# Output weights and results loaded a unit or more ahead of their split, keys stored regrouped, one bias sum for two column tiles

## The chip, the cores and the metric

The kernel runs on one core of one Trainium2 chip. The core has a TensorE (PE, with its weight loads shown apart as PEld), a VectorE (DVE), a ScalarE (ACT), a GpSimd (POOL) and a SyncE (SP) whose queue starts most transfers. Each engine executes its own instructions strictly in the order in which they stand in the program; between engines, semaphores make one wait for another. The metric is the device time in microseconds (us); lower is better.

## What is computed

One layer of an image backbone, on 1024 latent tokens (16 rows of 64 columns), 256 context tokens and 1024 features. A projection of the modulated input gives two parallel mixers; the output projection joins them.

```python
# 1. neighbourhood attention: 8 heads of 64, window of 8 rows x 16 columns, learned bias, plus all context keys
s_loc = jnp.einsum('bchd,bicjhd->bhcij', q_r, k_win).astype(jnp.float32) + bias
s_ctx = jnp.einsum('bchd,bnhd->bhcn', q_r, k_ctx).astype(jnp.float32)
s = jnp.concatenate([s_loc.reshape(B, H, GRID_W, kh * NA_KW), s_ctx], axis=-1)
p = jax.nn.softmax(s, axis=-1).astype(v.dtype)
...
# 2. gated DeltaNet: 4 heads of 128, chunked scan, forward and backward in time
v_new = u_n - jnp.einsum('bhcd,bhde->bhce', w_n, state)
o_n = (jnp.einsum('bhcd,bhde->bhce', q_n, state)
       + jnp.einsum('bhij,bhje->bhie', qk_n, v_new))
state = state * gl_n[..., None, None] + jnp.einsum('bhcd,bhce->bhde', k_n, v_new)
...
# 3. both gated, joined, projected; normalised residual
y = jnp.concatenate([o_na * jax.nn.silu(na_z), o_g * jax.nn.silu(g_z)], axis=-1) @ w_out
x = x + gate[:, None] * rmsnorm(y, g_post)
```

All arithmetic has the precision of fp32. Matrix products run as two or three products of operands that are split in a high and a low part, so each weight and each result is "split": ACT copies the rounded high part, another engine subtracts it from the original to get the low one.

## The kernel before

The program has two parts. Up to about 554 us come the projections, the convolution, the scan's triangular inverses and all that feeds the mixers; the change touches there only `qk_out`, which splits queries and keys of attention and stores them in `qk_dram`. The rest is `phase_b`, and it is the part of interest.

**Attention** (`na_attn`, `na_unit`) runs over 4 pairs of heads (p), 2 row tiles (rt) and 4 column tiles (ct): 32 units of 128 queries, two heads each. Per head of a unit: POOL adds relative bias and mask into `gm` (L676; 288 columns for ct 0 and 3, 384 for 1 and 2); TensorE makes scores with the context keys, `pc` (L684), and with the window's keys, `pl` (L688); DVE takes a maximum `mi` (L692) and adds the bias (L693, giving `pt` and `nm`); ACT takes the exponentials (L694, L695); TensorE transposes them (L697, L702), DVE and ACT copy them out (`tl` L699, `tcx` L704); TensorE makes the output `po` (L710, L715). `pc` and `pl` have two buffers each. After four units `po` is scaled by the gate in `zs` and the sums' reciprocal `rb`, which TensorE transposes as `prt` (L621). The keys lie row by row in `kk`, so the window of a unit is read as columns 64 elements apart.

**The scan** (`delta_scan`) runs over 4 heads (h), 10 chunks, both directions d together. A step is a chain: TensorE `pa` with the state (L1133), DVE `y` (L1134), TensorE with the inverse `tm` (L1138), ACT `vn` (L1140, L1142), TensorE with the decayed keys `kd` (L1144), DVE the new state `s` (L1147), and beside it two matmuls for the output, `pos` (L1152, L1153). POOL makes `kd` and `vb` (L1125, L1128). After the last step of a head its result `o` is squared (L1170), normalised, transposed as `ot` (L1182) and gated in `zg`.

**The output projection** (`phase4`) multiplies eight tiles of results m by eight tiles of output weights: 384 matmuls `py` of 512 columns (L1218 to L1220). The order of the tiles k is `W_ORDER = [3, 0, 1, 2, 4, 5, 6, 7]`; tile 3 is the last pair of attention, tile 7 the last head of the scan. Results of earlier pairs and heads come back from `m_dram` into `mr` and are split (ACT L1205); the last pair's is split from `zs` by `split_m` (L659, L660). The weights are split in pieces of 128x512 by `split_w`: a load into a raw buffer `wor`, of which there are two, an ACT copy (L647) and a POOL subtract (L648). Five tiles are split inside attention and the scan (`w_out_early`, into buffers `qh`, `ql`, `kk`, `o`, `tm` that are free by then), three in `phase4` (`fintm`, `finkq`, `wh`).

`phase_b` writes attention and scan interleaved: after unit u it has written min(43, 1.40 u) scan steps (a head is ten steps and a beginning and an end). That is only the order of writing. The program is then scheduled: a list scheduler with its own model of durations takes, for each engine, what it believes to be ready, and this fixes the order on each engine. Where buffers of two pools share addresses, the later user waits for the earlier.

Of the kernel before, what the change touches and what calls it, by code (L numbers as in the profile page):

```python
# [11 lines left out]
F32 = mybir.dt.float32  # L12
# [8 lines left out]
P = 128  # L21
# [118 lines left out]
class K:  # L140
    def __init__(self, tc, I, out, dbg=None):
        self.tc, self.nc, self.I, self.out = tc, tc.nc, I, out
        self.dbg = dbg or {}
        self.na_first = None
        self.gate = self.after = None
# [371 lines left out]
    def qk_out(self, p, i, gr, src):  # L517
        nc = self.nc
        n, scale, c0 = 512 if gr < 2 else CT, 1.0 if i else 0.125, S * i + 512 * gr
        src, rows = src[:, :n], slice(P * p, P * p + P)  # L520
        hi, lo = (self.wp.tile([P, 512], F32R, name=f"s{c}_{'qk'[i]}{p}{gr}", tag="st", bufs=4)[:, :n] for c in "hl")
        nc.scalar.activation(hi, src, AF.Copy, scale=scale)
        nc.vector.scalar_tensor_tensor(lo, src, scale, hi.bitcast(F32), ALU.mult, ALU.subtract)
        nc.sync.dma_start(self.qk_dram[0, rows, c0:c0 + n], hi.bitcast(F32))
        nc.sync.dma_start(self.qk_dram[1, rows, c0:c0 + n], lo.bitcast(F32))
# [59 lines left out]
    def na_attn(self, na, ps):  # L585
# [55 lines left out]
    def split_w(self, k, hi, lo):  # L641
        nc = self.nc
        hr, lr = hi.bitcast(F32R), lo.bitcast(F32R)
        for o in range(0, D, 512):
            raw = self.g3.tile([P, 512], F32, name=f"wor{k}_{o}", tag="wor", bufs=2)
            self.load(raw, self.I["w_out"][k * P:(k + 1) * P, o:o + 512], self.na_last)
            nc.scalar.copy(hr[:, o:o + 512], raw)  # L647
            nc.gpsimd.tensor_tensor(lr[:, o:o + 512], raw, hi[:, o:o + 512], ALU.subtract)  # L648
        self.wo[k] = (hr, lr)
# [13 lines left out]
    def na_unit(self, ps, p, rt, ct, qk, vv, gts, mk, sums, po):  # L663
# [7 lines left out]
        for hh in range(2):  # L671
# [3 lines left out]
            gm = self.nw.tile([P, 384], F32, name=f"gm{p}_{u}_{hh}", tag="gm", bufs=2)  # L675
            nc.gpsimd.tensor_tensor(gm[:, :n].rearrange("p (n c r) -> p n c r", c=nco, r=4), gv,  # L676
                                    mk[:, mo:mo + n].rearrange("p (n c r) -> p n c r", c=nco, r=4), ALU.add)
# [3 lines left out]
            pl3 = pl[:, :n].rearrange("p (n c r) -> p n c r", c=nco, r=4)  # L681
            qs, kk = qk[hh]
            for i, a in enumerate(qs):
                nc.tensor.matmul(pc, a[:, u * P:(u + 1) * P], kk[:, S:S + CT], start=(i == 0), stop=(i == 1))  # L684
            kv = kk[:, 256 * rt:256 * rt + 768].rearrange("p (n r c) -> p n c r", c=64, r=4)[
                :, :, KCOL0[ct]:KCOL0[ct] + nco, :]
# [8 lines left out]
            nc.scalar.activation(pt[:, 384:640], pc, AF.Exp, bias=nm, accum_out=sums[:, ct, hh, 1:2])  # L695
# [496 lines left out]
    def phase4(self, p4, ps, last):  # L1192
# [7 lines left out]
        for k in W_ORDER:  # L1200
            if k not in self.ms and k != 7:
                raw = raws[:, D * (k % 2):D * (k % 2) + D]
                mh, ml = (tl(c, k).bitcast(F32R) for c in ("mh", "ml"))
                nc.sync.dma_start(raw, self.m_dram[k * P:(k + 1) * P, :])
                nc.scalar.copy(mh, raw)  # L1205
                nc.vector.tensor_tensor(ml, raw, mh.bitcast(F32), ALU.subtract)
                self.ms[k] = (mh, ml)
            if k not in self.wo and k != 7:
                self.split_w(k, *late[k])
# [12 lines left out]
        for tg in range(0, 8, 4):  # L1222
# [101 lines left out]
    def phase_b(self):  # L1324
        tc = self.tc
        g3 = self.g3
        self.wos, self.wo, self.ms = [], {}, {}
# [66 lines left out]
```

## Time and profile before

| | |
|---|---|
| three runs | 906.75, 904.99, 906.35 us; median 906.35 |
| profiled execution | 904.01 us, span 902.3 us, mean granted TensorE clock 0.963 of full |
| projections and inverses | up to about 554 us |
| attention with the scan | 554 to 791.8 us |
| output projection | 791.8 to 895.3 us |
| normalisation and store of the last tile | 895.3 to 902.3 us |

The span is the time from the first to the last instruction of one profiled execution; 1.7 us lie around it. Rows of the profile name a line of the kernel, the engine, the operation, and output and input by their names in the program. In rows that group instructions, the number after x is their count, then follow the busy time in us, the mean duration in ns and, behind the second bar, the idle time of the engine just before them and who ended it. In rows of a timeline the first number is the start in us and the second the duration. Rows of windows have the busy time and count of each engine in turn, then the granted TensorE clock (PEclk), then the share of the DMA engines.

### The profile page before, as it was taken

The numbers are of one execution on the slowest core, as the hardware profiler recorded it, in microseconds if no ns is written. First come the engines' busy times: TensorE is split into PE (matmuls) and PEld (weight loads), VectorE is DVE, ScalarE is ACT, GpSimd is POOL, SyncE is SP. The second block draws the span as 40 slices with busy tenths as digits, with TensorE's granted clock in tenths as the row PEclk, the third lists the DMA queues.
The fourth block names the chain that finished last, engine by engine and source line by source line (L and its number), as shares of the span: only waits on it lengthen the run. The fifth ranks groups of instructions, "written<-read, shape, count | busy, mean of one in ns | idle before, by whom it ended". The sixth has DMA issues, their size and how long they took to land.

```text
span 902.3 us, 16602 instructions
## 1 busy us (share of the span) xinstructions
PE 848.5 (94%) x6082; PEld 708.7 (79%) x6082; DVE 537.6 (60%) x1179; ACT 416.2 (46%) x1165; POOL 369.6 (41%) x431
## 2 busy tenths in 40 slices
PE   6999999999999989998998998999999988998996
PEld 4688887887788767787887877888887876887785
DVE  3463454456545699689428634677777775662442
ACT  5262525545645445652334444555545656532310
POOL 1432322614543532455241124568557569423210
PEclk9999999999999989999998985999999998999898
DMA  9786432346355534733799699949387152132351
GB/s 343 257 290 228 150 107 74 114 157 199 89 198 185 138 122 151 216 99 112 249 265 265 219 281 413 267 117 296 141 208 272 48 183 76 47 117 94 108 183 60
DMA packets 95176, 160.98 MB, mean 178 GB/s; under 512 B 28581, under 2 KB 55542, under 8 KB 92918
## 3 DMA queue, kind: packets, MB, share of 16 engines
q1 hardware_dynamic: 87606, 146.25, 51.2%
q10 hardware_dynamic: 7488, 13.67, 4.9%
q8 instruction: 48, 0.79, 0.4%
q14 instruction: 34, 0.28, 0.1%
HBM read 110.82 MB, written 52.42 MB: 181 GB/s over the span
## 4 chain that ended last, share of the span: by engine, by line
PE 64%; DVE 13%; DMA 9%; ACT 5%; issue 4%; POOL 2%; SPq 2%; ACTq 0%; DVEq 0%; POOLq 0%
PE py L1218 3%; PE py L1219 3%; PE py L1220 3%; DVE tb L1003 3%; PE pl L688 2%; DVE vb L1006 2%; PE po L715 2%; PE pl L697 2%; PE pz L464 2%; PE pc L684 2%; PE pz L460 2%; PE pz L465 2%; PE po L710 2%; PE pa L1138 2%; PE pa L1144 2%
## 5 line engine op out<-in xcount | busy, mean ns | idle before, releaser
L676 POOL TENSOR_TENSOR gm<-gt,mk 128x288 f32<-128x288 f32 (+1 forms) x64 | 64.3, 1009 | 36.0 <-DVE nm L693 35.9
L1125 POOL TENSOR_SCALAR kd<-kt,kd 128x128 f32<-128x128 f32 x72 | 43.4, 606 | 35.3 <-PE pa L1144 33.7
L694 ACT ACTIVATE pt<-pt,nm 128x288 f32<-128x288 f32 (+1 forms) x64 | 36.7, 574 | 35.7 <-DVE nm L693 35.5
L945 ACT ACTIVATE em<-em,gc 128x128 f32<-128x128 f32 x80 | 25.5, 391 | 38.2 <-DMA em<-gc_dram 32.3
L693 DVE CUSTOM_DVE_ANT_0 pt<-pl,gm,mi 128x288 f32<-128x288 f32 (+1 forms) x64 | 36.1, 564 | 11.5 <-PE pl L688 4.9
L699 DVE COPY tl<-pl 96x384 f32<-96x384 f32 (+1 forms) x64 | 35.3, 551 | 10.2 <-PE pl L697 9.9
L692 DVE TENSOR_REDUCE mi<-pc 128x1 f32<-128x256 f32 x64 | 26.8, 420 | 22.0 <-PE pc L684 21.1
L464 PE MATMUL pz<-hl,wh_gz 128*128 128x512 f32 x96 | 38.6, 402 | 0.0
L460 PE MATMUL pz<-hh,wh_gz 128*128 128x512 f32 x96 | 38.4, 400 | 0.0
L465 PE MATMUL pz<-hh,wl_gz 128*128 128x512 f32 x96 | 38.3, 399 | 0.0
L473 PE MATMUL pv<-wh_nv,hh 128*128 128x264 f32 x128 | 35.5, 295 | 2.5 <-ACT hh L262 1.7
L964 POOL TENSOR_SCALAR_AFFINE_SELECT qe<-qe 128x256 f32<-128x256 f32 x32 | 26.9, 840 | 25.8 <-DVE qe L963 25.8
L475 PE MATMUL pv<-wl_nv,hh 128*128 128x264 f32 x128 | 35.7, 286 | 1.5 <-POOL wl_nv L446 1.5
L474 PE MATMUL pv<-wh_nv,hl 128*128 128x264 f32 x128 | 36.5, 289 | 0.0
L1003 DVE TENSOR_TENSOR tb<-ab,vb 120x31 f32<-120x31 f32 (+15 forms) x62 | 32.1, 518 | 6.8 <-DMA ab<-ab_dram 5.1
L960 DVE SCALAR_TENSOR_TENSOR pm<-pk,beta,em 128x128 f32<-128x128 f32 x80 | 23.6, 343 | 19.9 <-PE pk L953 12.3
L697 PE MATMUL pl<-c,pt 128*96 128x128 f32 (+1 forms) x192 | 33.7, 285 | 1.4 <-ACT pt L694 1.2
L812 DVE SCALAR_TENSOR_TENSOR acc_v<-xp_v,cols,acc_v 128x1282 f32<-128x1282 f32 x16 | 27.5, 1719 | 9.0 <-ACT acc_v L810 8.9
L1138 PE MATMUL pa<-y,tm 128*128 128x128 f32 x144 | 29.1, 287 | 2.8 <-DVE y L1134 2.2
L1266 ACT ACTIVATE finv<-py 128x512 f32<-128x512 f32 x16 | 9.5, 599 | 46.8 <-PE py L1220 28.3
L1128 POOL TENSOR_SCALAR vb<-v,beta 128x128 f32<-128x128 f32 x40 | 24.2, 606 | 16.7 <-DVE y L1134 10.6
L704 ACT COPY tcx<-pc 128x256 f32<-128x256 f32 x64 | 23.8, 372 | 15.3 <-PE pc L702 15.1
(438 smaller groups left out, 2928.8 us busy)
## 6 DMA issues: line engine op xcount, KB each, us to landing
wada<-in_w_ada SPq DMA_DIRECT2D x16, 512.0 KB, 9.1
em<-gc_dram SPq DMA_DIRECT2D x20, 256.0 KB, 4.6
pm_dram<-pm SPq DMA_DIRECT2D x20, 256.0 KB, 3.3
pmf<-pm_dram SPq DMA_DIRECT2D x8, 640.0 KB, 8.0
tm_dram<-tm SPq DMA_DIRECT2D x8, 640.0 KB, 7.0
kk<-qk_dram SPq DMA_DIRECT2D x16, 320.0 KB, 7.9
tm<-tm_dram SPq DMA_DIRECT2D x4, 1280.0 KB
kq_dram<-kq SPq DMA_DIRECT2D x4, 1152.0 KB
```

The source lines that it names most:

```text
L460: r = nc.tensor.matmul(ps, wh, xh, start=(k == 0), stop=False)
L464: nc.tensor.matmul(ps, wh, xl, start=False, stop=False)
L465: nc.tensor.matmul(ps, wl, xh, start=False, stop=(k == KC - 1))
L474: nc.tensor.matmul(ps, xl, wh, start=False, stop=False)
L475: nc.tensor.matmul(ps, xh, wl, start=False, stop=(k == KC - 1))
L676: nc.gpsimd.tensor_tensor(gm[:, :n].rearrange("p (n c r) -> p n c r", c=nco, r=4), gv, mk[:, mo:mo + n].rearrange("p (n c r) -> p n c r", ...
L693: nc.vector.tensor_tensor_reduce(pt[:, :n], pl[:, :n], gm[:, :n], -1.0, mi, ALU.add, ALU.min, nm)
L694: nc.scalar.activation(pt[:, :n], pt[:, :n], AF.Exp, bias=nm, scale=-1.0, accum_out=sums[:, ct, hh, 0:1])
L697: nc.tensor.transpose(pl[:m, rc * P:(rc + 1) * P], pt[:, rc * m:(rc + 1) * m], self.ident)
L1003: nc.vector.tensor_tensor(t3, bc(ab[:, 0:m, m:m + 1], [r, m, n]), bc(vb[:, m:m + 1, m:], [r, m, n]), ALU.mult)
L1125: nc.gpsimd.tensor_scalar(kd, kt_[:, t, :], self.kd[:, h, d, t:t + 1], None, ALU.mult)
L1138: nc.tensor.matmul(pa, tm[:, d, t, :], y, start=True, stop=True)
```

## The change

It does four things.

1. `qk_out` stores the latent part of the keys regrouped, so that the four rows of a column stand together, and `na_unit` reads its window as one contiguous run per group of rows. For that ACT and DVE read eight groups of 512 keys from PSUM in a strided order.
2. The bias sum `gm` is not made for ct 2; units ct 1 and ct 2 share that of ct 1. 48 sums are left of 64, and `gm` has three buffers instead of two.
3. `split_w` only lists the pieces of a weight tile. `load_pieces` keeps up to two raw pieces loaded ahead, and `split_piece` splits the oldest. It is called once after each unit, so that the pieces listed at the end of pair 2 are split one a unit in pair 3, and twice in `phase4`, with two and six pieces. Its ACT copy is ordered behind the last exponential written.
4. `phase4` loads four results ahead, into four buffers, and splits them by a generator that is advanced once a tile; the rest of the scan (`last`) is written ahead of the fifth tile instead of the sixth.

```diff
+        kv = lambda v, o: v.rearrange(f"p (n {o}) -> p n c r", r=4, c=64) if i and gr < 2 else v
+        nc.scalar.activation(kv(hi, "c r"), kv(src, "r c"), AF.Copy, scale=scale)
...
@@ na_attn: after each unit
+                    self.split_piece()
                     yield
...
     def split_w(self, k, hi, lo):
-        for o in range(0, D, 512):
+        self.wo[k] = (hi.bitcast(F32R), lo.bitcast(F32R))
+        self.pieces.extend((k, o, hi[:, o:o + 512], lo[:, o:o + 512]) for o in (0, 512))
+        self.load_pieces()
+
+    def load_pieces(self):
+        while self.pieces and len(self.staged) < 2:
+            k, o, hi, lo = self.pieces.pop(0)
             raw = self.g3.tile([P, 512], F32, name=f"wor{k}_{o}", tag="wor", bufs=2)
             self.load(raw, self.I["w_out"][k * P:(k + 1) * P, o:o + 512], self.na_last)
-            nc.scalar.copy(hr[:, o:o + 512], raw)
-            nc.gpsimd.tensor_tensor(lr[:, o:o + 512], raw, hi[:, o:o + 512], ALU.subtract)
+            self.staged.append((raw, hi, lo))
+
+    def split_piece(self, n=1):
+        for _ in range(min(n, len(self.staged) + len(self.pieces))):
+            raw, hi, lo = self.staged.pop(0)
+            self.order(nc.scalar.copy(hi.bitcast(F32R), raw), self.last_exp)
+            nc.gpsimd.tensor_tensor(lo.bitcast(F32R), raw, hi, ALU.subtract)
+            self.load_pieces()
...
@@ na_unit
-            gm = self.nw.tile([P, 384], F32, name=f"gm{p}_{u}_{hh}", tag="gm", bufs=2)
+            if ct != 2:
+                self.gm[hh] = self.nw.tile([P, 384], F32, name=f"gm{p}_{u}_{hh}", tag="gm", bufs=3)
...
+            gm = self.gm[hh]
...
+            kv = kk[:, 256 * rt:256 * rt + 768].rearrange("p (n f) -> p n f", f=256)[
+                :, :, 4 * KCOL0[ct]:4 * KCOL0[ct] + m]
...
@@ phase4
+        raws = [raws[:, :D], raws[:, D:]] + [p4.tile([P, D], F32, name=f"mr{i}") for i in range(2)]
...
+        for i in range(4):
+            load_m(i)
...
+                self.order(nc.scalar.copy(mh, raw), self.last_exp)
...
+                parts = split_in()
+                for _ in range(2):
+                    next(parts)
+                self.split_piece(2)
                 for i, k in enumerate(W_ORDER[:6]):
+                    next(parts, None)
...
-                    if i == 5:
+                    if i == 4:
                         for _ in last:
                             pass
+                        self.split_piece(6)
```

In the changed file the lines of attention stand 19 to 21 further down (`gm` L695, `pc` L704, `pl` L708, transposes L718 and L723, `po` L731 and L736), those of the scan 21 (`pa` L1154, L1159, L1165, `pos` L1173, L1174, `ot` L1203), the split pieces are at L664 and L665, the splits of results at L676 and L1234, `py` at L1249 to L1251.

The scheduler makes another order of it. Three places follow. On **TensorE at the start of attention**, behind the eight score matmuls of unit 0 of pair 0, before:

```order
L1138 MATMUL pa_0_5883<-v_5781,tm_5783 128x128
L1138 MATMUL pa_1_5884<-vb_1_1_5896,tm_5783 128x128
L697 MATMUL pl_0_0_5725<-c_60,pt_0_0_5732 96x128 x3
L702 MATMUL pc_0_0_5724<-c_60,pt_0_0_5732 128x128 x2
L1144 MATMUL pa_0_5883<-vn_0_0_5888,kd_0_0_5886 128x128
L697 MATMUL pl_0_1_5749<-c_60,pt_0_1_5756 96x128 x3
L702 MATMUL pc_0_1_5748<-c_60,pt_0_1_5756 128x128 x2
L688 MATMUL pl_1_0_5798<-kk_0_5266,qh_0_5269 128x384
L688 MATMUL pl_1_0_5798<-kk_0_5266,ql_0_5272 128x384
L1144 MATMUL pa_1_5884<-vn_1_1_5898,kd_1_1_5894 128x128
```

The same place of the changed kernel: between the score matmuls and these rows stand 46 scan matmuls of head 0 (`pa`, `pos`), and the rows are the last of 54 and what comes then.

```order
L1174 MATMUL pos_5885<-vn_0_5_6214,qe_5784 128x128
L1165 MATMUL pa_1_5884<-vn_1_6_6231,kd_1_6_6224 128x128
L1154 MATMUL pa_0_5883<-s_0_5_6218,kq_5780 128x128
L1154 MATMUL pa_1_5884<-s_1_6_6235,kq_5780 128x128
L1173 MATMUL pos_5885<-s_1_7_6130,kq_5780 128x128
L1174 MATMUL pos_5885<-vn_1_6_6231,qe_5784 128x128
L1159 MATMUL pa_0_5883<-y_0_6_6301,tm_5783 128x128
L1159 MATMUL pa_1_5884<-y_1_5_6318,tm_5783 128x128
L718 MATMUL pl_0_0_5725<-c_60,pt_0_0_5732 96x128 x3
L723 MATMUL pc_0_0_5724<-c_60,pt_0_0_5732 128x128 x2
L1165 MATMUL pa_0_5883<-vn_0_6_6304,kd_0_6_6299 128x128
L708 MATMUL pl_1_0_5798<-kk_0_5266,qh_0_5269 128x384
```

So the first transposes of attention have moved behind 54 scan matmuls instead of two. On POOL the first two bias sums stood ahead of the scan's first `kd` and `vb`, and stand behind 22 of these now. The third buffer of `gm` makes attention's pool 1536 bytes a partition longer, and its end now shares addresses with a buffer of the phase before.

On **ACT at the end of attention**, from the first exponential of the last unit's second head, before:

```order
L694 ACTIVATE pt_7_1_9073,sums_1_8735<-pt_7_1_9073,nm_7_1_9072 128x288
L695 ACTIVATE pt_7_1_9073,sums_1_8735<-pc_7_1_9065,nm_7_1_9072 128x256
L1156 ACTIVATE o_8396<-pos_8409,egc 128x128
L704 COPY tcx_7_1_9085<-pc_7_1_9065 128x256
L1142 COPY vn_1_5_8849<-pa_1_8408 128x128
L1156 ACTIVATE o_8396<-pos_8409,egc 128x128
L1140 ACTIVATE vn_0_7_8922<-pa_0_8407,beta 128x128
L1156 ACTIVATE o_8396<-pos_8409,egc 128x128
L659 CAST m_9132<-zs_7616 128x1024
L1142 COPY vn_1_4_8939<-pa_1_8408 128x128
L1205 CAST mh_9144<-mr 128x1024
```

and in the changed kernel:

```order
L714 ACTIVATE pt_7_1_9039,sums_1_8695<-pt_7_1_9039,nm_7_1_9038 128x288
L715 ACTIVATE pt_7_1_9039,sums_1_8695<-pc_7_1_9031,nm_7_1_9038 128x256
L664 CAST wo_o_8357<-wor_512_8883 128x512
L664 CAST wo_tm_8358<-wor_0_9118 128x512
L725 COPY tcx_7_1_9051<-pc_7_1_9031 128x256
L664 CAST wo_tm_8358<-wor_512_9120 128x512
L676 CAST m_9100<-zs_7600 128x1024
L1234 CAST mh_9129<-mr 128x1024
L1234 CAST mh_9134<-mr 128x1024
```

The scan's copies are gone from this place (the scan has ended before). Three weight pieces (`wor`) stand ahead of the cast of `m` that the first matmul of the projection needs, and the last of them uses the raw buffer of the first.

On **TensorE in the last units of attention**, the transposes of the last head's result, in the changed kernel (pair 3, units 6 and 7):

```order
L718 MATMUL pl_6_0_8918<-c_60,pt_6_0_8925 128x128 x3
L723 MATMUL pc_6_0_8917<-c_60,pt_6_0_8925 128x128 x2
L1203 MATMUL ot_0_9267<-c_60,o_8356 128x128 x4
L704 MATMUL pc_7_0_9007<-kk_0_7573,qh_0_7576 128x256
L704 MATMUL pc_7_0_9007<-kk_0_7573,ql_0_7579 128x256
L708 MATMUL pl_7_0_9008<-kk_0_7573,qh_0_7576 128x288
L708 MATMUL pl_7_0_9008<-kk_0_7573,ql_0_7579 128x288
L1203 MATMUL ot_1_9274<-c_60,o_8356 128x128 x4
L718 MATMUL pl_6_1_8940<-c_60,pt_6_1_8947 128x128 x3
```

Before, they stood in the projection, behind seven of the eight products of its first six tiles, and with them 24 matmuls of the scan's last steps:

```order
L1220 MATMUL py_1_9199<-finkq,mh_9185 128x512
L1220 MATMUL py_1_9201<-finkq,mh_9185 128x512
L1220 MATMUL py_1_9203<-finkq,mh_9185 128x512
L1182 MATMUL ot_0_9338<-c_60,o_8396 128x128 x4
L1182 MATMUL ot_1_9345<-c_60,o_8396 128x128 x4
L1218 MATMUL py_1_9376<-wo_qh_8296,m_9132 128x512
L1219 MATMUL py_1_9376<-wo_qh_8296,m_9132 128x512
```

In the changed kernel the scan's last matmul is at unit 4 of pair 3, and units 3 to 7 of that pair have only a few scan matmuls among them.

More of the change, by code (lines that the diff above doesn't have):

```diff
@@ L1199, in phase4, with split_in @@
         raws = self.pf.tile([P, 2 * S], F32, name="mr", tag="vv")
-        for k in W_ORDER:
-            if k not in self.ms and k != 7:
-                raw = raws[:, D * (k % 2):D * (k % 2) + D]
+        raws = [raws[:, :D], raws[:, D:]] + [p4.tile([P, D], F32, name=f"mr{i}") for i in range(2)]
+        ms = [k for k in W_ORDER if k not in self.ms and k != 7]
+        load_m = lambda i: nc.sync.dma_start(raws[i % 4], self.m_dram[ms[i] * P:(ms[i] + 1) * P, :])
+        for i in range(4):
+            load_m(i)
+        for k in W_ORDER[:-1]:
+            if k not in self.wo:
+                self.split_w(k, *late[k])
+        def split_in():
+            for i, k in enumerate(ms):
+                raw = raws[i % 4]
                 mh, ml = (tl(c, k).bitcast(F32R) for c in ("mh", "ml"))
-                nc.sync.dma_start(raw, self.m_dram[k * P:(k + 1) * P, :])
-                nc.scalar.copy(mh, raw)
+                self.order(nc.scalar.copy(mh, raw), self.last_exp)
                 nc.vector.tensor_tensor(ml, raw, mh.bitcast(F32), ALU.subtract)
                 self.ms[k] = (mh, ml)
-            if k not in self.wo and k != 7:
-                self.split_w(k, *late[k])
+                if i + 4 < len(ms):
+                    load_m(i + 4)
+                yield
         banks = {"sc": 2, "sl": 2, "po": 1, "pa0": 1, "pa1": 1, "os": 1}
@@ L1326, in phase_b @@
         g3 = self.g3
-        self.wos, self.wo, self.ms = [], {}, {}
+        self.wos, self.wo, self.ms, self.pieces, self.staged = [], {}, {}, [], []
         def scans(ps):
```

22 lines of the change are left out of this document (11 added, 11 removed).

## Prediction

> **What bounds the kernel now.** I read the totals of the page first, then the windows by stage, then the lines of the stages that the change touches. On the page TensorE is busy for 94% of the span and holds most of the chain that ended last:
>
> ```profile
> span 902.3 us, 16602 instructions
> PE 848.5 (94%) x6082; PEld 708.7 (79%) x6082; DVE 537.6 (60%) x1179; ACT 416.2 (46%) x1165; POOL 369.6 (41%) x431
> PE 64%; DVE 13%; DMA 9%; ACT 5%; issue 4%; POOL 2%; SPq 2%; ACTq 0%; DVEq 0%; POOLq 0%
> ```
>
> So the time is the sum of TensorE's work, its idle time, and what it loses at a lower clock. The change adds no TensorE work. What can change is where it idles, and this must be read by stage: attention and scan run together up to 791.8 us, the output projection follows.
>
> ```profile
> core 0: us, PE busy (x) PEld busy (x) DVE busy (x) ACT busy (x) POOL busy (x), PEclk, DMA share, GB/s
> 560.00:735.00 175.00, 167.68 (x1481) 146.58 (x1481) 129.99 (x407) 96.03 (x357) 108.93 (x148) 1.00 0.65 192
> 735.00:758.00 23.00, 20.41 (x183) 16.79 (x182) 14.94 (x48) 15.91 (x59) 19.59 (x23) 1.00 0.49 161
> 758.00:761.20 3.20, 1.41 (x10) 0.94 (x9) 1.42 (x4) 0.62 (x1) 3.20 (x5) 1.00 0.00 0
> 761.20:768.00 6.80, 6.49 (x30) 5.34 (x32) 3.55 (x9) 3.95 (x12) 5.73 (x6) 0.50 0.24 78
> 768.00:791.80 23.80, 22.73 (x209) 19.90 (x207) 16.08 (x52) 14.27 (x48) 10.65 (x16) 1.00 0.12 45
> ...
> 826.00:832.00 6.00, 5.52 (x26) 4.23 (x24) 0.81 (x3) 4.27 (x18) 3.33 (x4) 1.00 0.71 247
> 832.00:836.35 4.35, 1.51 (x9) 0.84 (x8) 2.04 (x3) 0.00 (x0) 1.34 (x2) 0.99 0.06 21
> 836.35:843.10 6.75, 5.91 (x15) 4.64 (x15) 2.96 (x2) 2.08 (x3) 2.55 (x2) 0.50 0.18 66
> ```
>
> In the steady part (560 to 735) TensorE is idle for 7.3 of 175 us. While output weights are split (735 to 768) POOL is almost never free, and TensorE is idle for 2.6 + 1.8 + 0.3 us, with 1.1 more up to 791.8; after the nearly idle 758 to 761 its clock is 0.50 for 6.8 us. In the projection there is one hole (0.5 + 2.8 + 0.8 us idle), again with 6.75 us at 0.50 behind it. These two places are what the change can win.
>
> **Gains.** (a) *The weight split.* One 256 KB piece costs ACT 0.62 us and POOL 1.28, and each load took 3.7 us, because a load began only when the split two pieces before had freed its buffer:
>
> ```profile
> L647 ACT CAST wo_o<-wor 128x512 fp32r<-128x512 f32 x2 | 1.2, 618 | 2.2 <-DMA wor<-in_w_out 2.2
> 739.57 1.28 POOL L648 TENSOR_TENSOR wo_ql<-wor,wo_qh 128x512 fp32r<-128x512 f32 x1 [2.70 <-ACT wo_qh L647]
> wor<-in_w_out SPq DMA_DIRECT2D x16, 256.0 KB, 3.7
> ```
>
> With one piece a unit, loaded a unit before, a load has a unit's 7.3 us (worked out in d) to land. The idle time 2.6 + 1.8 + 0.3 + 1.1 = 5.8 goes, and of the 6.49 us of work at half clock most of half, 2.5: **-8.3**. What the end of attention has in its place is priced below. At least 4 should go.
>
> (b) *The hole in the projection.* It is the last head's result: TensorE waits for `o`, which waits for the scan's end, eight squares and a norm on POOL.
>
> ```profile
> PE ot L1182 <- DVE o L1179: 2.0, 1, 2.0
> ```
>
> In the changed order the scan ends some five attention units earlier, and both groups of `ot` transposes stand inside attention. Idle 0.5 + 2.8 + 0.8 = 4.1 goes, and 5.91 / 2 = 3.0 of half clock: **-7.1** (at least 4.1).
>
> (c) *Contiguous keys.* Rows for the same operands by shape, and a contiguous one of 512 columns:
>
> ```profile
> L684 PE MATMUL pc<-kk,ql 128*128 128x256 f32 x53 | 15.0, 284 | 0.0
> L688 PE MATMUL pl<-kk,ql 128*128 128x384 f32 x28 | 10.5, 374 | 0.0
> L688 PE MATMUL pl<-kk,ql 128*128 128x288 f32 x26 | 8.4, 324 | 0.0
> L1220 PE MATMUL py<-wo_ql,mh 128*128 128x512 f32 x7 | 2.9, 407 | 0.0
> ```
>
> From 256 to 512 contiguous columns a matmul grows by 123 ns, 0.48 ns a column. By that 288 would take 299 ns and 384 345; the strided ones take 25 and 29 more. There are 64 of each (32 units, two heads of 16 units a shape, two matmuls): 64 x 0.025 + 64 x 0.029 = 3.5; the ends of matmuls are modelled and not all of it lies on the path, so I take **-2.4**, range 0 to -4.8. The Trainium skill, "SBUF — State Buffer", section "Door 1", says that each fp32 access on a new 16-byte line pays a penalty, which would let one expect a larger gain; the rows here show under a tenth of a matmul, and the measurement decides. The regrouping itself costs eight strided reads of 512 PSUM columns on ACT and on VectorE, in the projections, where TensorE does not wait for them; I take nothing (0 to +2).
>
> (d) *Shared bias sums.* 16 of 64 go, each near the 1.0 us of this row:
>
> ```profile
> L676 POOL TENSOR_TENSOR gm<-gt,mk 128x288 f32<-128x288 f32 (+1 forms) x64 | 64.3, 1009 | 36.0 <-DVE nm L693 35.9
> ```
>
> That is 16 us of POOL, but POOL idled before these very sums, waiting for the buffer. TensorE's 7.3 us of steady idle can shrink a little: I take -1.3 (0 to -4). About as much is lost where the first piece of the fourth weight tile must wait behind the gate's results going out and back over DMA (+1.3, 0 to +3.7); the two cancel.
>
> **Losses.** (e) *The start.* In the changed order (shown above) TensorE has eight attention matmuls, then 54 scan matmuls, about 6.5 steps of both directions, and only then the first transposes of attention; POOL makes 22 scan operations before the first bias sum. A scan step is a chain, here with little in its way:
>
> ```profile
> 571.68 0.34 DVE L1147 SCALAR_TENSOR_TENSOR s<-s,egl,pa 128x128 f32<-128x128 f32 x1
> ...
> 573.18 0.39 PE L1138 MATMUL pa<-y,tm 128*128 128x128 f32 x2
> ...
> 573.66 0.37 ACT L1140 ACTIVATE vn<-pa,beta 128x128 f32<-128x128 f32 x1 [0.24 <-PE pa L1138]
> ...
> 574.18 0.46 PE L1144 MATMUL pa<-vn,kd 128*128 128x128 f32 x2 [0.17 <-ACT vn L1140]
> 574.67 0.35 DVE L1147 SCALAR_TENSOR_TENSOR s<-s,egl,pa 128x128 f32<-128x128 f32 x1 [0.50 <-PE pa L1144]
> ```
>
> From state to state 574.67 - 571.68 = 3.0 us; some 0.2 of it is L1138 behind other work, so 2.8. TensorE's own work in it is 8.3 matmuls (54 / 6.5) at the 0.22 us between starts of these:
>
> ```profile
> 782.87 0.39 PE L1144 MATMUL pa<-vn,kd 128*128 128x128 f32 x2
> 783.10 0.39 PE L1152 MATMUL pos<-s,kq 128*128 128x128 f32 x2
> ```
>
> 1.8 us. One unit's attention used to fill the other 1.0. Half a step overlaps the first units: 6 x 1.0 = **+6.0** (0 if attention's operands on the other engines overlap more than the order lets me see).
>
> (f) *The last five units* have almost no scan left beside them. A unit took (786.65 - 561.42) / 31 = 7.3 us with its share of the scan:
>
> ```profile
> 561.42 0.66 PE L710 MATMUL po<-tcx,vcx 128*64 128x128 f32 x8
> ...
> 786.65 0.66 PE L710 MATMUL po<-tcx,vcx 128*64 128x128 f32 x8
> ...
> 787.89 0.49 PE L1152 MATMUL pos<-s,kq 128*128 128x128 f32 x2
> ```
>
> The program gives a unit 1.4 scan steps, of ten matmuls at 0.22 in the middle of a scan, 3.1 us; with 0.3 idle a unit (7.3 of 175 us) attention's own work is 7.3 - 0.3 - 3.1 = 3.9 us a unit. But a score buffer, of which there are two and each unit fills both, goes through this chain:
>
> ```profile
> L692 DVE TENSOR_REDUCE mi<-pc 128x1 f32<-128x256 f32 x64 | 26.8, 420 | 22.0 <-PE pc L684 21.1
> L693 DVE CUSTOM_DVE_ANT_0 pt<-pl,gm,mi 128x288 f32<-128x288 f32 (+1 forms) x64 | 36.1, 564 | 11.5 <-PE pl L688 4.9
> L694 ACT ACTIVATE pt<-pt,nm 128x288 f32<-128x288 f32 x30 | 16.0, 533 | 14.7 <-DVE nm L693 14.7
> L695 ACT ACTIVATE pt<-pc,nm 128x256 f32<-128x256 f32 x62 | 28.5, 460 | 0.0
> L704 ACT COPY tcx<-pc 128x256 f32<-128x256 f32 x63 | 23.4, 371 | 15.3 <-PE pc L702 15.1
> ```
>
> 0.42 + 0.56 + 0.53 + 0.46 + 0.37 = 2.3, with some 2.5 for its matmuls, transposes and the two sum read-outs: 4.8, so 0.9 idle a unit, **+4.5** for five (1 to 7).
>
> (g) *From attention to projection.* ACT's order behind the last exponential is now: two pieces, `tcx`, the next piece, and only then the cast of `m` that the first projection matmul reads. That third piece needs a raw buffer freed by the first one's POOL subtract, and then its own load: 0.62 + 1.28 + 3.7 + 0.62 + 1.05 (the cast, in the row below) = 7.3 us.
>
> ```profile
> L1205 ACT CAST mh<-mr 128x1024 fp32r<-128x1024 f32 x6 | 6.3, 1050 | 10.3 <-DMA mr<-m_dram 10.0 <-DVE m L660 0.3
> ```
>
> TensorE has 2.2 us of work in it (`po` 787.89 - 786.65 = 1.24, and some 1.0 of transposes), no scan any more; with 2.0 idle ahead, while the last unit's scores go through the chain of (f), that is 7.1 idle. So long a hole brings the half clock as the one at 832 did: +3.0. Together **+10.1** (4 to 12).
>
> **Sum:** -8.3 - 7.1 - 2.4 + 6.0 + 4.5 + 10.1 = **+2.8 us**, with (d) at nothing. Against the profiled execution (span 902.3 us and 1.7 around it, 904.0) that is 906.8; the median of the runs shown, 906.35, lies 2.3 above that execution, so I forecast 909.1, said as **909**.
>
> **Rivals.** *The clock stays low at the start* (slower). The idle hole at 527 to 532 gave half clock up to 559.9 although TensorE was busy for most of it, and the scan alone now starts inside that stretch:
>
> ```profile
> 386.00:388.00 2.00, 0.92 (x7) 0.93 (x8) 1.04 (x2) 0.51 (x1) 1.02 (x1) 1.00 0.26 66
> 532.50:559.90 27.40, 23.68 (x349) 21.92 (x347) 9.75 (x23) 10.30 (x29) 8.02 (x11) 0.50 0.97 368
> ```
>
> Then TensorE's share of a step doubles and the step goes from 2.8 to about 4: six steps, +7, **916**. Against it: at half clock a step has 3.7 us of work, so TensorE is nearly always busy and should get its clock back; and at 386 it kept full clock with 0.92 of 2.00 busy. The Trainium skill, "TensorE: Matmul & The Clock Gate", section "HAM oscillation — how this bites in real kernels", allows holes up to about 3.4 us, and its Part 1 has the clock back after about as much sustained work: by that this rival is out and the clock term of (g) is half as large. The trace agrees on the hole (836.35 follows one) but took 6.75 us to come back.
>
> *The closing holes are short* (faster). If the third piece's load is issued early enough, or takes 2 us, TensorE idles in pieces under some 2.5 us and keeps its clock: (g) is then 4 and (f) 2. For it: nothing else of attention's end gets longer, and the loads of this stretch meet an emptier queue than the one that took 3.7. It decides from about 3 us less idle. -6.1 - 2.5 from the sum: **900.5**.
>
> *Loading ahead does not remove the waits* (does not do what it says). POOL is busy for 28.5 of 33 us between 735 and 768, so its queue may be the cause and not the load: 16 POOL sums less are spread over all of attention. Then (a) is 4: **913**.
>
> **How the numbers follow.** The forecast has 45%; its own range of about 4 us either way gives 17 to "within 0.2%", 5 to faster, 23 to slower. (0.2%, 1.8 us, is about what a measurement of this kernel can tell from no change.) Low clock 13% (slower), short closing holes 30% (faster), waits that stay 12% (10 slower, 2 the same). Faster 35, same 19, slower 46. The range from 898 to 919 takes in all four with the bounds of (a), (e) and (g) that are likely together.
>
> **What would show it.** (e): a stretch near 557 to 575 with scan matmuls only and TensorE 60 to 70% busy; wrong if attention's transposes stand within it. (a): no `wor` wait on ACT before the last units. (b): no `ot` after the first `py`, and no 0.50 in the projection. (f), (g): idle of some 10 us in the last 40 us ahead of `py`, and a half-clock stretch just behind its start. (c): `pl` at 299 and 345 ns. The forecast is wrong if the start costs nothing, or if `m` is cast ahead of the third piece's load.

## Result and the profile after

| | us | ratio to before, 95% interval |
|---|---|---|
| before, six runs | 904.95 median (903.87 to 906.75) | |
| changed kernel, six runs | 912.12 median (909.08 to 915.14) | 1.0075 (1.0053 to 1.0096) |
| its profiled execution | 912.89, span 911.1 | 904.01, span 902.3 before |

The changed kernel is slower by 7 us. The forecast was 909 in a range of 898 to 919, "slower" the likeliest. The page after, its first lines and the row of the bias sums:

```profile
span 911.1 us, 16603 instructions
PE 855.2 (94%) x6082; PEld 713.8 (78%) x6082; DVE 534.8 (59%) x1179; ACT 417.0 (46%) x1165; POOL 355.2 (39%) x415
...
L695 POOL TENSOR_TENSOR gm<-gt,mk 128x288 f32<-128x288 f32 (+1 forms) x48 | 46.4, 974 | 28.1 <-DVE nm L713 27.9
```

POOL works 14.4 us less, and TensorE is "busy" 6.7 us longer with the same 6082 matmuls, at a mean granted clock of 0.954 (before 0.963). The windows after, cut at events that both traces have: the first `pc`, the first transposes of attention, `po` of the last unit of pair 2, the first `py`.

```profile
557.22:579.64 22.42, 20.15 (x118) 16.60 (x117) 11.41 (x38) 6.67 (x22) 12.38 (x20) 0.90 0.96 330
579.64:745.27 165.63, 159.20 (x1418) 140.20 (x1417) 124.45 (x395) 95.85 (x363) 97.64 (x135) 0.99 0.61 173
745.27:797.40 52.13, 45.55 (x396) 38.24 (x395) 38.56 (x111) 30.17 (x109) 24.90 (x30) 0.99 0.34 109
797.40:811.95 14.55, 9.93 (x59) 7.46 (x59) 5.36 (x12) 6.34 (x17) 5.39 (x5) 0.50 0.27 84
811.95:817.50 5.55, 5.55 (x13) 4.39 (x14) 5.53 (x5) 4.35 (x5) 0.73 (x1) 0.50 0.85 320
817.50:904.13 86.63, 86.63 (x372) 69.54 (x371) 23.02 (x39) 15.52 (x37) 14.17 (x20) 1.00 0.30 100
```

The hole in the projection is gone: 86.63 of 86.63 us busy at full clock. In its place stand a start of 22.4 us and a stretch of 20 us at half clock around the end of attention. The same stages of before (the first row takes in the start):

```profile
554.23:726.40 172.17, 165.13 (x1436) 144.47 (x1435) 126.91 (x397) 95.14 (x354) 107.52 (x144) 0.98 0.67 200
726.40:791.59 65.19, 59.15 (x495) 50.18 (x494) 42.37 (x129) 38.28 (x133) 43.70 (x54) 0.95 0.31 106
```

Between these events the order moves scan matmuls, so the plain difference must be corrected by 0.22 us for each of them that a stage gained or lost (0.4 for each group of `ot`). The scan counts are those of the orders. The `ot` of the third head have moved ahead of the last `po` of pair 2 (735 to 739 us; before at 765 to 769), and those of the last head ahead of the first `py`.

| stage | before | after | difference | of it moved work | net | forecast |
|---|---|---|---|---|---|---|
| up to the first `pc` | 554.2 | 557.2 | +3.0 | 0 | +3.0 | 0 |
| to the first transposes | 3.0 | 22.4 | +19.4 | +11.4 (52) | **+8.0** | +6.0 |
| to the last `po` of pair 2 | 169.2 | 165.6 | -3.5 | -0.7 (7 less, two `ot`) | -2.8 | -3.1 |
| to the first `py` | 65.2 | 66.7 | +1.5 | -4.6 (21 less) | **+6.1** | +4.0 |
| to the last `py` | 103.7 | 92.2 | -11.5 | -6.1 (24 less, two `ot` less) | **-5.4** | -4.1 |
| tail | 7.0 | 7.0 | 0 | 0 | 0 | 0 |

(The forecast column sorts the terms: (e) in the second row, three quarters of (c), for three of four pairs, and the gain of (d) in the third, the rest of (c), (a), (f), the idle time of (g) and the loss of (d) in the fourth, (b) and the clock of (g) in the fifth.) The 3.0 us of the first row lie ahead of everything that the change reorders. In 14 profiled executions of this study the first `pc` stands anywhere from 554.2 to 559.4; before has the earliest. With the old keys it was 554.2 to 556.2 (4 executions), with the regrouped ones 554.9 to 559.4 (10). The ranges overlap; whether a microsecond of it is the change's stays open.

The start, on TensorE, first and last rows and one step of the scan between them:

```profile
557.22 0.58 PE L704 MATMUL pc<-kk,qh 128*128 128x256 f32 x1
...
571.16 0.49 PE L1154 MATMUL pa<-s,kq 128*128 128x128 f32 x2 [0.18 <-DVE s L1168]
...
572.93 0.46 PE L1165 MATMUL pa<-vn,kd 128*128 128x128 f32 x2 [0.28 <-POOL vb L1149]
...
574.50 0.49 PE L1154 MATMUL pa<-s,kq 128*128 128x128 f32 x2 [0.18 <-DVE s L1168]
...
579.64 0.53 PE L718 MATMUL pl<-c,pt 128*96 128x128 f32 x3
```

Twenty microseconds of scan alone, as the order said. A step takes 574.50 - 571.16 = 3.34 us, not 2.8. In these rows TensorE waits 0.28 us of it for `vb` from POOL and 0.18 for the state from DVE; that the two directions of the scan follow each other on the engines may be the rest, but is not shown apart.

### The profile page after: what moved, and what is told of

Same layout as the page of the kernel before. It is cut to its first block, busy times and chain, and to the rows that moved or that the text cites. A ratio compares the mean times of both kernels' runs of the same rounds, so it can differ in the third digit from the quotient of the medians.

```text
span 911.1 us, 16603 instructions
## 1 busy us (share of the span) xinstructions
PE 855.2 (94%) x6082; PEld 713.8 (78%) x6082; DVE 534.8 (59%) x1179; ACT 417.0 (46%) x1165; POOL 355.2 (39%) x415
## 5 line engine op out<-in xcount | busy, mean ns | idle before, releaser
L695 POOL TENSOR_TENSOR gm<-gt,mk 128x288 f32<-128x288 f32 (+1 forms) x48 | 46.4, 974 | 28.1 <-DVE nm L713 27.9
L1304 DVE TENSOR_TENSOR finv<-py,ggb 128x512 f32<-128x512 f32 x16 | 11.0, 690 | 56.1 <-ACT finv L1303 56.0
L718 PE MATMUL pl<-c,pt 128*96 128x128 f32 (+1 forms) x192 | 33.3, 284 | 6.5 <-ACT pt L714 6.5
L981 DVE SCALAR_TENSOR_TENSOR pm<-pk,beta,em 128x128 f32<-128x128 f32 x80 | 23.5, 343 | 18.7 <-PE pk L974 11.3
```

The source lines that it names most:

```text
L695: nc.gpsimd.tensor_tensor(self.gm[hh][:, :n].rearrange("p (n c r) -> p n c r", c=nco, r=4), gv, mk[:, mo:mo + n].rearrange("p (n c r) -> p ...
L718: nc.tensor.transpose(pl[:m, rc * P:(rc + 1) * P], pt[:, rc * m:(rc + 1) * m], self.ident)
```

## Experiments

All ratios are to runs of the kernel before on the same chip (its median is 904.95 for the row of the changed kernel, and 904.0, 905.3 or 904.6 for the others). "pc to py" and "py to end" are from one profiled execution each, net of moved scan work as above.

| kernel | median us | ratio (95%) | pc to py, net | py to end, net |
|---|---|---|---|---|
| changed kernel | 912.1 | 1.0075 (1.0053, 1.0096) | +11.3 | -5.4 |
| changed, two `gm` | 896.7 | 0.9914 (0.9883, 0.9945) | -2.1 | -5.5 |
| before, three `gm` | 920.8 | 1.0180 (1.0142, 1.0218) | +20.2 | -7.8 |
| changed, `m` first | 909.9 | 1.0068 (1.0043, 1.0092) | +10.8 | -5.6 |
| two `gm`, `m` first | 897.8 | 0.9927 (0.9892, 0.9962) | -2.1 | -6.0 |
| two `gm` and a pad | 908.6 | 1.0037 (1.0012, 1.0062) | +10.7 | -6.5 |
| three `gm`, three `tl` | 896.8 | 0.9913 (0.9883, 0.9944) | -2.9 | -6.4 |
| keys alone | 901.1 | 0.9964 (0.9942, 0.9985) | -4.4 | 0.0 |
| two `gm`, no sharing | 897.7 | 0.9919 (0.9890, 0.9948) | -0.8 | -7.8 |
| loading ahead alone | 897.0 | 0.9902 (0.9866, 0.9938) | -0.2 | -7.8 |
| sharing alone | 900.4 | 0.9953 (0.9929, 0.9977) | -0.9 | -7.1 |
| `m`, then squares | 896.7 | 0.9904 (0.9869, 0.9938) | -6.0 | -6.7 |
| weights ahead of the gate | 892.1 | 0.9855 (0.9820, 0.9890) | -7.9 | -6.4 |

### Two bias buffers in the changed kernel

```diff
-                self.gm[hh] = self.nw.tile([P, 384], F32, name=f"gm{p}_{u}_{hh}", tag="gm", bufs=3)
+                self.gm[hh] = self.nw.tile([P, 384], F32, name=f"gm{p}_{u}_{hh}", tag="gm", bufs=2)
```

> The changed kernel with two bias buffers (gm) instead of three, so that attention's pool no longer shares addresses with the inverse's buffer. Its order on TensorE has the first transposes of attention behind 2 scan matmuls again (54 in the changed kernel), and the scan lasts to the end of attention. Theory (the time is lost at the start and in the last units, because of the third buffer): some 6 us at the start and 4 in the last units come back, 902 us (899 to 905), no stretch of scan alone after 557. Rival (the staged split or the regrouped keys themselves cost the time): 910 to 914, as the changed kernel.

896.7: 15 us less than the changed kernel and 7 less than before, more than the theory said. The first transposes stand 2.8 us behind the first `pc`. One number of the change turns a gain into a loss.

### A third bias buffer in the kernel before

```diff
-            gm = self.nw.tile([P, 384], F32, name=f"gm{p}_{u}_{hh}", tag="gm", bufs=2)
+            gm = self.nw.tile([P, 384], F32, name=f"gm{p}_{u}_{hh}", tag="gm", bufs=3)
```

> The kernel before with one number changed: three bias buffers instead of two; nothing else. Its order has 54 scan matmuls ahead of attention's first transposes. Theory (the third buffer moves the start): 6 us are lost at the start, a part comes back because only 2 scan matmuls are left behind the start of the projection (24 before): 908 to 911. Rival (the start's order is harmless, its idle time is filled by what is taken from later): 905, as the kernel before.

920.8, slower than the changed kernel and than the 908 to 911 expected. The start is the same 22.55 us. The rest is in pair 3 (windows of this kernel):

```profile
556.17:578.72 22.55, 19.96 (x117) 16.58 (x116) 11.28 (x38) 6.56 (x22) 12.43 (x20) 0.90 1.00 348
...
749.15:783.35 34.20, 24.76 (x162) 19.19 (x162) 14.18 (x40) 16.41 (x51) 18.88 (x18) 0.79 0.41 131
```

TensorE is idle for 9.4 of 34 us there, and for a part at half clock. In its order the scan stands still for the first units of pair 3 (295 scan matmuls since the first `pc` are done when that pair begins, and still 295 three units later), just while the old weight split holds up ACT (8.6 us of waits for `wor` from 749 to 784). That these waits lie open because scan work was shifted to the start is argued and not shown: 57 scan matmuls were still to come, and the scheduler placed them later. My expectation had put any such loss at nothing.

### Is it the buffer or its address?

A pad of the third buffer's size beside two buffers, and three buffers with one `tl` less:

```diff
+                self.nw.tile([P, 384], F32, name="pad", tag="pad", bufs=1)
...
-                self.gm[hh] = self.nw.tile([P, 384], F32, name=f"gm{p}_{u}_{hh}", tag="gm", bufs=3)
+                self.gm[hh] = self.nw.tile([P, 384], F32, name=f"gm{p}_{u}_{hh}", tag="gm", bufs=2)
```

> The changed kernel with two bias buffers and an unused tile of the third one's size (1536 bytes a partition) in the same pool. Theory (it is the addresses: the longer pool reaches into the inverse's buffer, and the scheduler puts attention's first steps behind it): as the changed kernel, 910 to 914. Rival (the third buffer itself, which lets POOL run ahead with bias sums and get in the scan's way): as with two buffers, 897.

```diff
-            tl = self.nw.tile([P, 384], F32, name=f"tl{p}_{u}_{hh}", tag="tl", bufs=4)
+            tl = self.nw.tile([P, 384], F32, name=f"tl{p}_{u}_{hh}", tag="tl", bufs=3)
```

> The changed kernel with its three bias buffers, and three buffers instead of four for the transposed probabilities (tl), which makes the pool as long as before. Theory (addresses): the start as in the kernel before, 897 (895 to 900), up to 3 us more if the fourth tl buffer mattered. Rival (the third buffer itself): 910 to 914.

The pad, which nothing writes or reads, brings back the 54 scan matmuls, a start of 22.6 us and 908.6 us; three buffers in a pool of the old length take 896.8. So it is the pool's length and not the third buffer. (The pad's median lies 3.5 us under that of the changed kernel. Its ten runs reach from 905.6 us at a mean granted clock of 0.968 to 914.3 at 0.957; why the two kernels differ isn't shown.)

### The cast of m ahead of the last pieces

```diff
-        nc.scalar.copy(hi.bitcast(F32R), z)
+        cast = nc.scalar.copy(hi.bitcast(F32R), z).ins.name
+        if k == 3:
+            self.last_exp = cast
```

> The changed kernel with the last two weight pieces ordered behind the cast of m instead of the last exponential; the start is as in the changed kernel. Theory (the third piece's load and copy hold up the cast of m): the first projection matmul comes 2 to 3 us sooner after the last exponential, and with the lower clock behind it 3 to 5 us are won, 908 us. Rival (the hole is attention's own chain at the end, without scan beside it): within 1 us of the changed kernel, 911 to 913.

> Both edits on the changed kernel: two bias buffers, and the last two weight pieces behind the cast of m. Theory: the two losses are separate, 898 to 901, faster than the kernel before. Rival (with two buffers the cast of m already stands ahead of the third piece): the same as with two buffers alone.

Nothing that can be told apart: 909.9 against 912.1 (ratios 1.0068 and 1.0075), 897.8 against 896.7. From the last `po` to the first `py` the changed kernel has 811.95 - 806.64 = 5.31 us, this one 812.20 - 806.90 = 5.30. ACT of the changed kernel shows why:

```profile
809.69 0.62 ACT L664 CAST wo_tm<-wor 128x512 fp32r<-128x512 f32 x1 [3.10 <-DMA wor<-in_w_out]
810.85 1.04 ACT L676 CAST m<-zs 128x1024 fp32r<-128x1024 f32 x1 [0.54 <-DVE zs L630]
```

The third piece does come late and ACT does wait for its load, but it is done at 810.3, and the cast begins only when DVE has gated the result, 0.5 us later. The load lies inside attention's own closing chain. The rival holds. With two buffers the other rival does: there the cast of `m` (795.01 us) already stands ahead of the third piece (795.94).

### The parts one by one

Regrouped keys alone, on the kernel before (with the subtract of `qk_out` in the changed form):

```diff
+        nc.scalar.activation(kv(hi, "c r"), kv(src, "r c"), AF.Copy, scale=scale)
...
+            kv = kk[:, 256 * rt:256 * rt + 768].rearrange("p (n f) -> p n f", f=256)[
+                :, :, 4 * KCOL0[ct]:4 * KCOL0[ct] + m]
```

> The kernel before with only the keys regrouped; the order on every engine is that of before. Theory by the rows of before (25 to 29 ns a matmul): 902 to 903, 2.4 us less, and 299 and 345 ns for the pl rows. Rival (the moving operand's stride costs TensorE nothing, the rows differ by what stands around them): 905, with the same durations as before.

```profile
L693 PE MATMUL pl<-kk,ql 128*128 128x384 f32 x23 | 7.8, 338 | 0.0
L693 PE MATMUL pl<-kk,ql 128*128 128x288 f32 x22 | 6.5, 297 | 0.0
```

297 and 338 ns, against 324 and 375 in the same stretch of before: 27 and 37 ns a matmul. The rows with `qh` gain 20 and 34 (398 and 442 before, 378 and 408 here). Times 32 each that is 3.8 us; the median is 4.2 us under before. The hole in the projection stays as it was (12.82 of 17.00 us busy, clock 0.81).

On the changed kernel, a sum for every tile in two buffers; and, as the second of these runs, the keys in the old order as well (the diff of keys alone, reversed), so that only loading ahead is left:

```diff
-            if ct != 2:
-                self.gm[hh] = self.nw.tile([P, 384], F32, name=f"gm{p}_{u}_{hh}", tag="gm", bufs=3)
-                nc.gpsimd.tensor_tensor(self.gm[hh][:, :n].rearrange("p (n c r) -> p n c r", c=nco, r=4), gv,
...
-            gm = self.gm[hh]
+            gm = self.nw.tile([P, 384], F32, name=f"gm{p}_{u}_{hh}", tag="gm", bufs=2)
+            nc.gpsimd.tensor_tensor(gm[:, :n].rearrange("p (n c r) -> p n c r", c=nco, r=4), gv,
```

> The changed kernel with two bias buffers and a sum for every column tile (64 sums), so keys regrouped and pieces and results loaded ahead without the shared sums. Theory (POOL was not the bound, the sums saved bring about 1 us): 898, 1 to 2 us above the version with two buffers and sharing. Rival (the sums saved are what takes POOL's queue out of the way of the weight split): 902 or more.

> The changed kernel with two bias buffers, 64 bias sums and the keys in the old order, so that pieces and results loaded ahead are all that differs from the kernel before. Theory (the gain of the regrouped keys, 3 to 4 us by their own run, adds to that of loading ahead): 900 to 902. Rival (loading ahead brings nothing by itself, the gain of the version without sharing is the keys'): 904 to 906.

Sharing alone, on the kernel before with its two buffers:

```diff
-            gm = self.nw.tile([P, 384], F32, name=f"gm{p}_{u}_{hh}", tag="gm", bufs=2)
+            if ct != 2:
+                self.gm[hh] = self.nw.tile([P, 384], F32, name=f"gm{p}_{u}_{hh}", tag="gm", bufs=2)
...
+            gm = self.gm[hh]
```

> The kernel before with only the shared bias sums, in two buffers (48 sums instead of 64). Its scan ends earlier, with 6 matmuls behind the start of the projection instead of 24. Theory (the sums themselves are worth about 1 us, what is moved by them more): 902 to 905. Rival (POOL's queue bounds the weight split): 899 to 901.

Loading ahead alone takes 897.0, no more than the version with all three parts: here my theory (that the keys' gain adds to it) was wrong by 4 us. Sharing alone takes 900.4. The two right-hand columns of the table tell why these two don't add. Loading ahead alone wins 0.2 us up to the first `py` and 7.8 behind it; sharing alone 0.9 and 7.1. Both let the scan all but end inside attention (2 and 6 scan matmuls are left behind the first `py` instead of 24), and that closes the hole in the projection. It can be closed once. (The time of sharing alone lies in the range of its rival, that POOL's queue bounds the weight split; but its gain lies behind the split, and pair 3 idles more than before, 8.9 us against 6.0.)

For the keys this is no answer, since they win 4.4 us ahead of the first `py` and nothing behind it. Beside loading ahead (two `gm`, no sharing) they win 2.5 us up to the last `po` of pair 2 (169.17 us from the first `pc`, 171.66 without them) and lose 1.8 in pair 3 (72.22 us at a granted clock of 0.93, against 70.38 at 0.98). These are single executions; why the clock is lower there is not shown.

### What else was left

```diff
-            nc.scalar.activation(sq, o[:, t, :], AF.Square, accum_out=var[:, t:t + 1])
+            r = nc.scalar.activation(sq, o[:, t, :], AF.Square, accum_out=var[:, t:t + 1])
+            if h == 3:
+                self.order(r, self.last_exp)
```

> The version with two bias buffers, and ACT's last two weight pieces and the eight squares of the last head ordered behind the cast of m. With two buffers the trace had m's cast behind the eight squares, and TensorE waited 3.5 us for it. Theory: the first projection matmul comes 3 us sooner and the clock drops for a shorter time, 893 (891 to 895). Rival (the result of attention is not there sooner, or the later transposes of the last head open a new hole): 896 to 898.

```diff
-            self.load(zs, self.z_dram[P * p:P * p + P, :])
             self.na_last = self.last_load
+            self.load(zs, self.z_dram[P * p:P * p + P, :])
```

> As the version with the squares behind the cast of m, and the weight pieces may be loaded ahead of the last pair's gate (zs), whose load waits for the result before it to leave its buffer. With two buffers ACT stood 3.5 us in front of the first piece's copy, and TensorE 3.3 us for the exponential behind it. Theory: that hole goes, 2 to 4 us less than without this edit. Rival (the loads then meet others, and the wait moves to the gate): no difference.

Both start from the version with two `gm` and `m` first. The first brings no difference in time (896.7), though its profiled execution has the first `py` 2.5 us behind `prt` instead of 4.2. The second, with both edits, takes 892.1: the fastest kernel of the study, 12.5 us under before. All four of its runs lie below all four of the first; its profiled execution is the slowest of them (894.9) and the other's the fastest (895.3), so the two traces show less of the gain than the medians. In the version with two buffers ACT stood in front of its first piece, and TensorE behind it (its waits from 735 us):

```profile
ACT wo_qh L664 <- DMA wor<-in_w_out: 3.5, 1, 3.5
...
PE pl L718 <- ACT pt L714: 5.0, 5, 3.3
PE py L1249 <- ACT m L676: 3.5, 1, 3.5
```

With the squares behind the cast of `m`, the wait of `py` is down and the other two are still there:

```profile
ACT wo_qh L664 <- DMA wor<-in_w_out: 2.5, 1, 2.5
...
PE pl L720 <- ACT pt L716: 4.5, 6, 2.4
PE py L1253 <- ACT m L676: 1.9, 1, 1.9
```

The load of the last pair's gate (`zs`) waits until the result before it has left its buffer, and the weights were told to load behind the gate. With the weights ahead of it ACT no longer waits for the first piece, and TensorE has left:

```profile
PE pl L720 <- ACT pt L716: 2.6, 5, 1.1
PE py L1253 <- ACT m L676: 1.9, 1, 1.9
```

## Why the prediction came out right

The direction comes from terms that held: the losses (e) and the holes of (f) and (g), the gains (b) and (c). That 909 lies so near 912 is in part luck. (a) was too good by 8 us, and (f) with (g) too bad by some 6, and these nearly cancel. The forecast also started from the median of three runs, 906.35, where six runs give 904.95: the change itself was forecast at +2.8 us and measured +7.2. The rival with waits that stay, 913, lies nearer than the forecast.

- **(e) the start, +6.0.** Right in kind, by the order alone; 8.0 measured. The step was mis-sized twice: it takes 3.34 us against 2.8, and in the middle of the scan it has ten matmuls (571.16 to 574.50), 2.2 us of work where 1.8 was taken. So its idle time, 1.1 us, is near the 1.0 of the forecast because the two errors offset, and 6.5 such steps make 7.4 of the 8.0. The cause, the pool's length, is shown by the pad.
- **(a) the weight split, -8.3.** This step failed. "The idle time 2.6 + 1.8 + 0.3 + 1.1 = 5.8 goes" did not happen: with loading ahead alone TensorE idles for 8.0 us from the last `po` of pair 2 to the first `py` (62.41 of 70.38 us busy) where before it idled for 6.0, and 0.2 us are won up to that `py`. In the changed kernel ACT's waits for loads became one of 3.0 us for the first piece (3.5 with two buffers), because it is loaded behind the gate, and one of 3.1 at the end that nothing waits for. I had seen that wait, priced it at +1.3 and set it against (d). The rival that loading ahead does not remove the waits had the right result and the wrong cause: POOL is not full in the changed kernel (24.9 of 52 us), the load is late. The edit that lets the weights pass the gate shows it, on the version with two buffers. With loading ahead alone the idle time is spread over short waits, the longest 1.0 us, so the late load is not the most of it there; what is stays open.
- **(b) the hole in the projection, -7.1.** Right: no `ot` behind the first `py`, 86.63 of 86.63 us busy, and 7.1 to 7.8 won by each of two parts alone. My reason was incomplete: not the moved `last` or the start's order is needed, a scan that ends a few steps sooner is enough.
- **(c) regrouped keys, -2.4.** Right in kind and too low: 296 and 337 ns in the changed kernel, where 299 and 345 were forecast; 4.2 us alone. Beside loading ahead that gain did not last, as said above. The 512-column row that gave the slope was too steep a guide (0.48 ns a column; from 288 to 384 it is 0.43).
- **(d) shared sums, nothing.** With two buffers the version without sharing is 0.9 us slower, within its interval. Sharing alone wins 4.2 us; its trace has most of the gain behind the first `py`, where the scan that ends sooner leaves no hole. I had not seen that.
- **(f) and (g), +14.6.** The forecast of some 10 us idle in the last 40 ahead of `py` and of a half-clock stretch came true: 9.4 us idle from 771.95 to 811.95, and clock 0.50 from 797.4 to 817.5. But the chain that (g) named, the third piece's load, is not the one that ends last: the runs with the cast of `m` first gain nothing. The hole is attention's own closing chain (exponential, transposes, `po`, `prt`, the gate on DVE), which lies open because no scan is left. That in turn is the start's price: 54 matmuls done ahead are 54 that cannot fill these units. With two buffers the scan lasts to the last unit, and (e), (f) and a part of (g) go together: 15 us. The last 40 us ahead of the first `py`, before, changed, and changed with two buffers, have 3.8, 9.4 and 6.0 us idle (of the last, 3.5 are the wait of `py` for `m` behind the squares) and mean clocks of 0.91, 0.82 and 0.98:

```profile
751.59:791.59 40.00, 36.19 (x296) 30.88 (x294) 26.00 (x77) 22.02 (x70) 25.61 (x32) 0.91 0.16 53
...
771.95:811.95 40.00, 30.65 (x230) 23.19 (x226) 25.15 (x64) 21.61 (x73) 16.09 (x16) 0.82 0.24 77
...
756.09:796.09 40.00, 34.04 (x310) 30.01 (x308) 28.79 (x91) 24.67 (x87) 18.91 (x24) 0.98 0.28 94
```

The rival of short closing holes had its condition and not its outcome. TensorE's longest gap in those 40 us is 1.9 us, but the clock fell all the same, at 797.17, behind 3.42 us with 2.08 busy and no gap above 0.62. Nor does the trace of before agree that a hole of up to 3.4 us is free, as the prediction reads it: the clock fell at 836.30 behind gaps of 2.00 and 0.84 us.

The rival of a low clock at the start did not come about: full clock was back by 563.5, with TensorE busy 3.99 of 4.30 us until then and 12.85 of 14.60 from 565 on.

```profile
559.20:563.50 4.30, 3.99 (x17) 2.92 (x16) 1.29 (x4) 1.08 (x4) 2.35 (x4) 0.71 1.01 416
...
565.00:579.60 14.60, 12.85 (x86) 10.56 (x84) 8.93 (x30) 5.37 (x18) 9.05 (x15) 1.00 0.94 282
```

From the first `pc` on the sum was +2.8 and the two executions differ by 5.9: the start cost 2.0 more than forecast, the stage behind it won 0.3 less, the end of attention cost 2.1 more, the projection won 1.3 more. Within the end of attention (a) was too good by about 8, if loading ahead is worth there what it is worth alone, and (f) and (g) were then too bad by some 6; the table cannot part them further, since they share the same units.

## What to carry to other kernels

When one edit grows a pool, look at which earlier pool's addresses its end now reaches, and at the order of each engine, before looking at what the buffer is for: 1536 bytes a partition that nothing used cost more than the change won. A gain that closes a hole can be had only once, so measure parts alone and together before adding them. Work that runs beside a long chain is a filler; ask where it will be missing when it is done sooner.

## What the runs showed of the hardware

The granted clock changed only at the ends of steps of 3.41 us. It was 0.50 from 836.30 to 843.13 in the kernel before, two such steps, and from 797.17 to 817.65 in the changed one, six. Here are steps of the changed kernel, then of before:

```profile
793.75:797.17 3.42, 2.08 (x11) 1.23 (x11) 3.42 (x9) 1.76 (x6) 0.01 (x1) 1.00 0.01 2
...
810.82:814.23 3.41, 2.28 (x5) 1.82 (x6) 2.30 (x2) 2.99 (x4) 0.86 (x1) 0.50 0.80 312
814.23:817.65 3.42, 3.42 (x9) 2.64 (x8) 3.40 (x4) 2.46 (x4) 0.88 (x1) 0.50 0.78 269
...
832.89:836.30 3.41, 1.26 (x8) 0.84 (x8) 2.04 (x3) 0.00 (x0) 0.45 (x2) 1.00 0.00 0
836.30:839.71 3.41, 2.56 (x7) 2.03 (x7) 1.91 (x2) 2.08 (x3) 2.55 (x2) 0.50 0.00 0
839.71:843.13 3.42, 3.42 (x9) 2.65 (x9) 1.05 (x1) 0.00 (x0) 0.00 (x0) 0.50 0.35 132
```

The clock was lost behind a step with many small gaps as well as behind one with a hole. Over the 14 traces of this study it was lost only behind steps in which TensorE was busy for at most 68%, and came back only behind steps with at least 82%; the share alone does not decide, since some steps of 44% kept the full clock, and full steps of 32x32 and 64x64 matmuls (532.52 to 539.34 before) did not bring it back. The Trainium skill, "TensorE: Matmul & The Clock Gate", Part 1, has the full clock back after a busy window of about 3.4 us and calls that window free-running. The trace agrees: work without a gap went on for 5.7 us (from 811.95) and 5.9 us (from 837.20) until the clock rose, because it began inside a step, and the first step that it filled was the last at 0.50.

Reading PSUM in regrouped order cost ACT and VectorE nothing: the key splits of 128x512 took 590 and 685 ns, and the contiguous ones of before 591 and 686.

```profile
L525 ACT ACTIVATE sh_k<-pk 128x512 fp32r<-128x512 f32 x8 | 4.7, 590 | 3.9 <-PE pk L466 3.9
L527 DVE TENSOR_TENSOR sl_k<-pk,sh_k 128x512 fp32r<-128x512 f32 x8 | 5.5, 685 | 4.4 <-ACT sh_k L525 3.6 <-DMA v_dram<-vt 0.7
L522 ACT ACTIVATE sh_k<-pk 128x512 fp32r<-128x512 f32 x8 | 4.7, 591 | 3.4 <-PE pk L465 3.4
L523 DVE SCALAR_TENSOR_TENSOR sl_k<-pk,sh_k 128x512 fp32r<-128x512 f32 x8 | 5.5, 686 | 4.9 <-ACT sh_k L522 4.0 <-ACT hh L259 0.9
```
